# A gap of 448 bytes in front of the tiles that hold the lower weight parts of two transformer blocks

## The chip, the core and the metric

The kernel runs on one core of one Trainium2 chip. The metric is the device time of one execution in microseconds (us). Three runs of the kernel before took 2190.77, 2190.84 and 2191.94 us; their median is 2190.84 us. One further execution was profiled; it took 2190.65 us.

The engines are named as in the profile: PE is TensorE's matrix multiplication and PEld its loading of the stationary operand, DVE is VectorE, ACT is ScalarE, POOL is GpSimd, SP is SyncE, whose queue issues the loads from device memory.

## The reference, cut to what matters

Two transformer blocks over 256 positions of width 2048, in float32, one after the other. The first mixes a gated convolution, a pooling branch and a cross attention to 256 memory rows; the second has two kinds of attention. Both end in a gated feed-forward part of width 5632. Nearly all arithmetic is in products of the activations with weight matrices that are read once:

```python
h = rmsnorm(x, g_mix[l]);  z = h @ w_in[l]
...
x = x + mix @ w_out[l]
h = rmsnorm(x, g_ffn[l])
u = causal_dwconv(h @ w_up[l], ffn_conv_w[l]) + ffn_conv_b[l]
gate, val = jnp.split(u, 2, axis=-1)
x = x + (jax.nn.silu(gate) * val) @ w_down[l]
...
h = rmsnorm_2(x, norm_attn[l]);  proj = h @ w_in[l]
...
x = x + jnp.concatenate([ya, yb], axis=-1) @ w_out[l]
h = rmsnorm_2(x, norm_ffn[l])
x = x + (jax.nn.silu(h @ w_gate[l]) * (h @ w_up[l])) @ w_down[l]
return rmsnorm_2(x, norm_final)
```

## The kernel before, in words

**Number format.** A float32 weight `w` is split into an upper part `hi`, the value rounded to the format of TensorE's fast float32 mode (`float32r`), and a lower part `lo = w - hi`. Activations are split in the same way, and the two parts of an activation lie side by side: a row of tile `A` (and of `M`, `mix`, `hid`, `y`, which share one place) is 16 chunks of 512 columns, 256 of the upper part and 256 of the lower part. A product is then `hi` times both activation parts plus `lo` times the upper activation part.

**Units.** Weights come in units of 16 blocks of 128 x 128 (1 MB). SP's queue loads a unit into a tile `raw`, three units ahead. ScalarE copies half a unit (128 x 1024) into a tile `hi` (line 175); VectorE subtracts and writes the tile `lo` (line 187). There are three `raw` tiles and four each of `hi` and `lo`.

**The two kinds of matmul in most units** (function `products`, called by `ws_units`): weights are stationary, activations move. A *long* (line 208) loads a block of `hi` and moves the 512 columns of a chunk; a *short* (line 211) loads the block of `lo` and moves the first 256 columns of the same chunk:

```python
def long(acc, hi, lo, x, first, last):
    mm(acc, lhsT=hi, rhs=x, start=first, stop=last)

def short(acc, hi, lo, x, first, last):
    mm(acc[:, S:], lhsT=lo, rhs=x[:, :S], start=False, stop=False)
```

Blocks go four at a time, and `products` turns the order round from one four to the next, so that eight longs and eight shorts follow one another, except where a sum opens or closes.

**V units** (function `vs_unit`, lines 275 to 277): for the value projections the roles are exchanged. The activation slice is stationary and 512 columns of `hi` or `lo` move: line 275 loads the upper activation part and moves `hi`, 276 loads the same and moves `lo`, 277 loads the lower activation part and moves `hi`.

**Order.** Everything is written out by hand in `emit_all`: for each quarter of a unit the splits, the work that is due on the other engines (`post`), then the quarter's matmuls, then small products of the attention (`extra`). No scheduler moves anything.

**Places.** Tiles are allocated pool by pool, in the order in which the pools are made: `cst`, `wraw`, `whi`, `wlo`, `big`, then the small ones. The blocks of `hi` and `lo` are 512 bytes wide in a partition and the chunks of the activation tiles 2048 bytes, so all blocks of a kind, and all chunks, have the same place modulo 512 bytes. `big` begins with a tile of 64 bytes, `home`, that nothing uses. In the built program of the kernel before the places modulo 512 are: `raw`, `hi` and `lo` 32; `X`, `A` and the tile of `M`, `mix`, `hid` and `y` 96; the work tiles of the pools behind it (`z`, `c`, `qk` and others) 160; the table of constants `kc` 128.

Of the kernel before, what the change touches and what calls it, by code (L numbers as in the profile page):

```python
# [10 lines left out]
F32 = mybir.dt.float32  # L11
# [7 lines left out]
P = 128  # L19
# [80 lines left out]
def tile_two_blocks(ctx: ExitStack, tc: tile.TileContext, a: dict, out: bass.AP):  # L100
    nc = tc.nc
    pool = lambda name, bufs, **kw: ctx.enter_context(tc.tile_pool(name=name, bufs=bufs, **kw))
    cst = pool("cst", 1)
    wraw_p = pool("wraw", 3)
    whi_p = pool("whi", 4)
    wlo_p = pool("wlo", 4)
    big = pool("big", 1)
    t1 = pool("t1", 14)
# [10 lines left out]
    ones = cst.tile([P, P], F32, name="ones")  # L119
    ident = kc[:, K_IDENT:K_IDENT + P]  # L120

    big.tile([P, 16], F32, name="home")
    X = big.tile([P, KT, S], F32, name="X")
    A = big.tile([P, KT, 2 * S], F32R, name="A")
# [1006 lines left out]
```

## Time and profile before

| what | value |
|---|---|
| time, median of 3 runs | 2190.84 us |
| the profiled execution | 2190.65 us |
| its span, first to last instruction | 2188.8 us |
| PE busy | 2169.9 us, 99% |
| PEld busy | 1896.8 us, 87% |
| DVE busy | 1600.6 us, 73% |
| ACT busy | 1143.9 us, 52% |
| chain that ended last, on PE | 97% |

The profile lists, for each group of equal instructions, how many there are, the busy time that they cover together and the mean duration of one. Matmuls are pipelined, so the durations of neighbours overlap, and the sum of durations is more than the time. What a matmul costs in a row of them is seen in the chain that ended last: there each piece is given the time up to the start of the next one.

### The profile page before, as it was taken

What the parts mean: (1) busy time and instruction counts of PE and PEld (TensorE: products, weight loads), DVE (VectorE), ACT (ScalarE), POOL (GpSimd) and SP (SyncE); (2) the same over time, 40 slices, a digit from 0 to 9 for tenths busy, and PEclk for the clock granted to TensorE, in tenths of its full rate; (3) what the DMA queues carried; (4) which work ended last, traced back from release to release, by engine and by line L of the source; (5) the groups of instructions that cost most, each with busy time, mean ns of one, the idle gap of its engine ahead of it and who ended that gap; (6) DMA issues with size and microseconds to landing.
All of it is one profiled execution on the core that took longest, in us unless ns stands there. A gap on an engine that the chain in (4) does not pass through costs nothing.

```text
span 2188.8 us, 31334 instructions
## 1 busy us (share of the span) xinstructions
PE 2169.9 (99%) x12426; PEld 1896.8 (87%) x12426; DVE 1600.6 (73%) x2553; ACT 1143.9 (52%) x1738; POOL 108.2 (5%) x114
## 2 busy tenths in 40 slices
PE   8999999999999999999999999999999999999997
PEld 7888888888888888888888888888888888888886
DVE  8877778886588758888779677786665666666666
ACT  6555556664466535665456655455543445344442
POOL 4100010000000000003100000010000000000012
PEclk9999999999999999999999999999999999999998
DMA  7555555555555555555544444555555555555553
GB/s 284 201 171 180 191 188 196 191 192 191 193 192 192 193 184 193 190 185 192 193 167 160 156 172 154 175 199 189 191 190 193 193 192 193 192 192 189 189 184 113
DMA packets 60195, 408.99 MB, mean 187 GB/s; under 512 B 6672, under 2 KB 8592, under 8 KB 11792
## 3 DMA queue, kind: packets, MB, share of 16 engines
q1 hardware_dynamic: 60048, 406.99, 53.9%
q8 instruction: 97, 1.59, 0.3%
q14 instruction: 50, 0.41, 0.0%
HBM read 404.86 MB, written 2.10 MB: 186 GB/s over the span
## 4 chain that ended last, share of the span: by engine, by line
PE 97%; DVE 1%; DMA 1%; issue 0%; ACT 0%; DVEq 0%; SPq 0%; ACTq 0%
PE acc L208 60%; PE acc L211 30%; PE acc L275 1%; PE acc L276 1%; PE acc L277 1%; PE s_ps L432 1%; DMA raw<-in_w_k 1%; DVE lo L187 0%; PE pT_ps L468 0%; PE o_ps L922 0%; PE o_ps L880 0%; DVE M L545 0%; DVE end L1000 0%; DVE M L546 0%; PE nps L344 0%; DMA mem<-in_mem 0%
## 5 line engine op out<-in xcount | busy, mean ns | idle before, releaser
L175 ACT ACTIVATE hi<-raw 128x1024 fp32r<-128x1024 f32 x758 | 800.1, 1058 | 580.1 <-PE acc L208 405.5
L187 DVE TENSOR_TENSOR lo<-raw,hi 128x1024 fp32r<-128x1024 f32 x758 | 931.8, 1237 | 144.7 <-ACT hi L175 133.0
L208 PE MATMUL acc<-A,hi 128*128 128x512 f32 x3776 | 957.2, 393 | 0.0
L208 PEld LDWEIGHTS acc<-A,hi 128*128 128x128 f32 x3776 | 673.3, 188 | 115.5 <-issue 1.0
L211 PEld LDWEIGHTS acc<-A,lo 128*128 128x128 f32 x3776 | 509.3, 188 | 40.9 <-issue 0.7
L211 PE MATMUL acc<-A,lo 128*128 128x256 f32 x3776 | 523.4, 279 | 0.0
L208 PE MATMUL acc<-hid,hi 128*128 128x512 f32 x1408 | 360.1, 392 | 0.0
L208 PEld LDWEIGHTS acc<-hid,hi 128*128 128x128 f32 x1408 | 250.5, 188 | 41.4
L416 ACT ACTIVATE z<-acc 128x256 f32<-128x256 f32 x244 | 91.9, 382 | 262.4 <-PE acc L208 262.0
L211 PEld LDWEIGHTS acc<-hid,lo 128*128 128x128 f32 x1408 | 195.4, 188 | 17.3
L211 PE MATMUL acc<-hid,lo 128*128 128x256 f32 x1408 | 199.7, 279 | 0.0
L742 DVE TENSOR_TENSOR X<-acc,X 128x256 f32<-128x256 f32 x128 | 54.0, 422 | 177.4 <-PE acc L208 177.3
L418 DVE TENSOR_TENSOR z<-acc,z 128x256 f32<-128x256 f32 x244 | 103.1, 423 | 95.3 <-ACT z L416 89.6
L717 DVE SCALAR_TENSOR_TENSOR c<-z,vec,c 128x255 f32<-128x255 f32 (+1 forms) x188 | 90.0, 480 | 5.1 <-ACT c L712 1.1
L406 DVE TENSOR_TENSOR hid<-hid 128x256 fp32r<-128x256 f32 x88 | 37.4, 425 | 76.3 <-ACT hid L404 76.3
L424 DVE TENSOR_TENSOR z<-z,R_ffn 128x256 f32<-128x256 f32 x176 | 75.0, 426 | 6.0
L208 PE MATMUL acc<-y,hi 128*128 128x512 f32 x256 | 65.5, 394 | 0.0
L319 POOL TENSOR_TENSOR sq_attn<-sq_attn,sqt 128x256 f32<-128x256 f32 x30 | 29.5, 994 | 701.6 <-ACT sqt L317 701.5
L208 PE MATMUL acc<-mix,hi 128*128 128x512 f32 x256 | 64.2, 392 | 0.0
L394 ACT ACTIVATE A<-X,vec 128x256 fp32r<-128x256 f32 x64 | 32.5, 508 | 57.8 <-DVE X L743 57.3
L743 DVE TENSOR_TENSOR X<-acc,X 128x256 f32<-128x256 f32 x128 | 54.3, 425 | 4.4
L397 DVE SCALAR_TENSOR_TENSOR A<-X,vec,A 128x256 fp32r<-128x256 f32 x64 | 51.1, 810 | 8.3 <-ACT A L394 8.3
(174 smaller groups left out, 1352.6 us busy)
## 6 DMA issues: line engine op xcount, KB each, us to landing
raw<-in_w_up SPq DMA_DIRECT2D x88, 1024.0 KB, 4.8
raw<-in_w_down SPq DMA_DIRECT2D x88, 1024.0 KB, 4.9
raw<-in_w_gu SPq DMA_DIRECT2D x88, 1024.0 KB, 4.9
raw<-in_w_out SPq DMA_DIRECT2D x32, 1024.0 KB, 4.9
raw<-in_w_in SPq DMA_DIRECT2D x22, 1024.0 KB, 4.9
raw<-in_w_qkb SPq DMA_DIRECT2D x16, 1024.0 KB, 4.8
raw<-in_w_qka SPq DMA_DIRECT2D x16, 1024.0 KB, 4.9
raw<-in_w_vb SPq DMA_DIRECT2D x8, 1024.0 KB, 4.8
```

The source lines that it names most:

```text
L175: nc.scalar.activation(hi[:, :n], raws[i][:, c0:c0 + n], AF.Copy)
L187: nc.vector.tensor_tensor(out=lo[:, :n], in0=raws[i][:, c0:c0 + n], in1=hi[:, :n].bitcast(F32), op=ALU.subtract)
L208: mm(acc, lhsT=hi, rhs=x, start=first, stop=last)
L211: mm(acc[:, S:], lhsT=lo, rhs=x[:, :S], start=False, stop=False)
L397: nc.vector.scalar_tensor_tensor(out=a[:, kt, S:], in0=x, scalar=g, in1=hi.bitcast(F32), op0=ALU.mult, op1=ALU.subtract)
L406: nc.vector.tensor_tensor(out=hl[:, S:], in0=src, in1=h.bitcast(F32), op=ALU.subtract)
L416: nc.scalar.activation(z, acc[:, S:], AF.Copy)
L418: nc.vector.tensor_tensor(out=z, in0=acc[:, :S], in1=z, op=ALU.add)
L424: nc.vector.tensor_tensor(out=d, in0=z, in1=R, op=ALU.mult)
L717: nc.vector.scalar_tensor_tensor(out=c[:, s:], in0=z[:, :S - s], scalar=w[2 - s], in1=c[:, s:], op0=ALU.mult, op1=ALU.add)
L742: nc.vector.tensor_tensor(out=dst, in0=acc[:, :S], in1=X[:, m, :], op=ALU.add)
L743: nc.vector.tensor_tensor(out=dst, in0=acc[:, S:], in1=dst, op=ALU.add)
```

## The change

A pool `gap` with one tile of 112 float32 values (448 bytes in a partition) is made between `whi` and `wlo`. Nothing reads or writes it. All that lies behind it moves by 448 bytes, which is 64 less modulo 512. In the built program the places modulo 512 are then: `raw` and `hi` 32, as before; `lo` 480; `X`, `A` and the tile of `M`, `mix`, `hid` and `y` 32; the work tiles behind them 96; `kc` 128, as before. So the chunks of the activations lie like the blocks of `hi`, and both lie 64 bytes behind the blocks of `lo`. Before, the chunks lay 64 bytes behind the blocks of `hi` and of `lo`. The instructions, their order on every engine and their waits are the same.

```diff
@@ -103,6 +103,7 @@
     cst = pool("cst", 1)
     wraw_p = pool("wraw", 3)
     whi_p = pool("whi", 4)
+    gap = pool("gap", 1)
     wlo_p = pool("wlo", 4)
     big = pool("big", 1)
     t1 = pool("t1", 14)
@@ -119,6 +120,7 @@
     ones = cst.tile([P, P], F32, name="ones")
     ident = kc[:, K_IDENT:K_IDENT + P]
 
+    gap.tile([P, 112], F32, name="gap")
     big.tile([P, 16], F32, name="home")
     X = big.tile([P, KT, S], F32, name="X")
     A = big.tile([P, KT, 2 * S], F32R, name="A")
```

## Rows read from the trace of the kernel before

**Rows 1.** The page: busy time (share) xinstructions, granted clock by slice, chain's shares; clock.
```profile
PE 2169.9 (99%) x12426; PEld 1896.8 (87%) x12426; DVE 1600.6 (73%) x2553; ACT 1143.9 (52%) x1738; POOL 108.2 (5%) x114
...
PEclk9999999999999999999999999999999999999998
...
PE 97%; DVE 1%; DMA 1%; issue 0%; ACT 0%; DVEq 0%; SPq 0%; ACTq 0%
...
core 0: 2188.8 us, clock 0.997
```

**Rows 2.** Chain, 200 to 1000 us, by line; line 208's, then line 211's counts there.
```profile
by line: PE acc L208 66.3%; PE acc L211 33.6%; PE nps L344 0.1%; PE nps L326 0.0%
...
200.00:1000.00 800.00, 581.87 (x2317) 412.86 (x2316) 1.00 0.55 191
...
200.00:1000.00 800.00, 320.08 (x2318) 313.93 (x2318) 1.00 0.55 191
```

**Rows 3.** Lines 208 and 211, whole span: xcount, duration in ns min/median/max, first and last start.
```profile
L208 PE MATMUL acc<-A,hi x3776: 387/392/586, 58.9 to 2095.4; 128*128 128x512 f32 x199
...
L208 PE MATMUL acc<-hid,hi x1408: 387/392/397, 494.2 to 2172.9; 128*128 128x512 f32 x176
...
L208 PE MATMUL acc<-poolHL,hi x14: 387/392/396, 195.9 to 223.4; 128*128 128x512 f32 x14
...
L211 PE MATMUL acc<-A,lo x3776: 275/279/467, 59.8 to 2094.6; 128*128 128x256 f32 x199
```

**Rows 4.** Chain, 1597 to 1603 us: start us, us up to the next piece, what.
```profile
1597.11 0.91 PE acc L211 x8
1598.02 1.83 PE acc L208 x8
1599.84 0.94 PE acc L211 x8
```

**Rows 5.** Chain, 1066 to 1072 us, inside V units: by line, number of pieces, two of them.
```profile
by line: PE acc L276 35.0%; PE acc L277 35.0%; PE acc L275 34.9%
27 pieces in order of time: start us, us, what
...
1067.09 0.24 PE acc L277
1067.32 0.23 PE acc L275
```

**Rows 6.** Lines 275 to 277, as in rows 3, and what line 276's engine waited for.
```profile
L275 PE MATMUL acc<-hi,A x128: 393/398/497, 1046.5 to 1247.0; 128*128 128x512 f32 x128
...
L276 PE MATMUL acc<-lo,A x128: 388/396/399, 1046.7 to 1247.2; 128*128 128x512 f32 x128
...
  DVE lo L187: 5.0, 3
...
L277 PE MATMUL acc<-hi,A x128: 390/394/399, 1047.0 to 1247.5; 128*128 128x512 f32 x128
```

**Rows 7.** Timeline near 1015 us, matmuls, then loads: start us, us, engine, line, what, xcount.
```profile
1015.07 1.07 PE L208 MATMUL acc<-hid,hi 128*128 128x512 f32 x4
...
1014.96 0.76 PEld L208 LDWEIGHTS acc<-hid,hi 128*128 128x128 f32 x4
1015.76 0.19 PEld L211 LDWEIGHTS acc<-hid,lo 128*128 128x128 f32 x1
```

**Rows 8.** Chain at three places, as in rows 4.
```profile
1092.99 0.23 PE acc L277
...
1045.72 0.93 PE acc L208 x4
...
1281.10 0.91 PE acc L208 x4
1282.02 0.86 PE o_ps L880 x4
```

**Rows 9.** The lower parts' subtraction: group, xcount, busy us, mean ns, idle before.
```profile
L187 DVE TENSOR_TENSOR lo<-raw,hi 128x1024 fp32r<-128x1024 f32 x757 | 930.8, 1238 | 144.7 <-ACT hi L175 133.0
```

## The prediction

> **What bounds the kernel now.** I read the page first: TensorE is busy for 99% of the span, the chain that ended last lies on it for 97%, and its granted clock is full, 2.4 GHz, in all slices but the last (mean share 0.997) [rows 1]. VectorE has 27% of the span free and ScalarE 48%. So a nanosecond is worth something only where it is a nanosecond per matmul, and the next view is the chain inside a stretch, which gives the pitch of the matmuls: the time from the start of one to the start of the next. In the 800 us from 200 to 1000, line 208 (the long products, 512 moving columns) holds 66.3% of the chain in 2,317 instructions and line 211 (the short ones, 256 columns) 33.6% in 2,318 [rows 2]. That is 530.4 us / 2,317 = 228.9 ns for a long one and 268.8 us / 2,318 = 116.0 ns for a short one. The recorded durations, 392 and 279 ns in the median [rows 3], are longer by 163 ns since neighbours overlap; only differences of them count.
>
> The pitch is not one fixed number. A run of eight longs takes 1.83 us, 229 ns each, but a run of eight shorts takes 0.91 us (114 ns) in one place and 0.94 us (118 ns) in another, with the same tiles and shapes [rows 4]. Single long matmuls lie between 387 and 397 ns in duration [rows 3]. Nothing else waits there: something inside the matmul step, about 5 ns to either side, is open to change, and by 5,774 longs (seven groups by moving tile, of which the two largest and the last stand in [rows 3]) and as many shorts, 1 ns on every long is 5.8 us, 0.26% of the time.
>
> A third kind of step gives the comparison I rest on. In the V units (lines 275 to 277) the same 512-column matmul runs with the roles exchanged: the weight tile moves and the activation tile is loaded. There 27 steps fill 104.9% of 6 us [rows 5], so 233.1 ns, 4.2 ns more than in line 208; their medians of 398, 396 and 394 ns against 392 say the same [rows 3, 6]. What differs in addresses: in line 208 the moving tile lies 64 bytes behind the tile that is loaded beside it (places 96 and 32 modulo 512), in the V units 64 bytes ahead of it (32 and 96).
>
> **Rule against row.** By those rows the time of equal steps differs by 4.2 ns. The Trainium skill ("SBUF — State Buffer", Who interferes with whom, and "TensorE: Matmul & The Clock Gate", Step-by-step: what each phase is for) says that TensorE has two independent read ports, one for the moving operand and one for the weight load, and that a load takes nothing from the running matmul. By that rule placement is worth nothing and the sum would be zero; the trace does not bear it out fully, though it also exchanges the roles of the tiles.
>
> **The change part by part.** The instructions and their order on every engine are the same in both programs; only addresses move. Beside each matmul runs the load for the next one: a load that stands before four longs starts at 1014.96, 0.11 us ahead of the first of them (1015.07), and the load for the short behind them at 1015.76, when the fourth long starts (1015.07 + 3 x 0.229) [rows 7]. So what counts is the place of the running moving tile against the next stationary tile.
>
> *Longs beside a load of an upper part.* Most longs stand in runs of eight, some in runs of four [rows 4, 8], so about 7/8 of the 5,774 loads of upper parts run beside a long: 5,052 (an estimate). Here the distance goes from 64 bytes to 0. No run of the trace has 0; single steps have it. The last long before a V unit reads the activation tile while a slice of an activation tile is loaded: the four longs that end in it take 0.93 us at 1045.72, and again at another such place [rows 8], 232 ns each, one of them alike. The last V step before a long run reads the weight tile while a weight tile is loaded: 0.23 us, inside the V units' alternation of 0.23 and 0.24 [rows 5, 8]. Both are between the two levels and none shows a gain. I take the middle of the two levels, +2.1 ns: 5,052 x 2.1 = +10.6 us. The ends: the V level for all, +4.2 ns, +21.2 us; below, the fastest single step (387 against 392 ns, -5 ns), -25 us, which no run of eight comes near; a third of that, -8 us, is as far as I find likely.
>
> *Shorts beside a load of an upper part*, the other eighth, 722: distance 64 to 0. Their two levels are 114 and 118 around a mean of 116; I take 0, with ends of -2 x 722 = -1.4 and +2 x 722 = +1.4 us.
>
> *Everything beside a load of a lower part* (7/8 of the shorts, 1/8 of the longs): moving tile and lower tile both shift by -64 modulo 512 and keep their distance; 0. The one opening is the level that a run of shorts falls into, which is set at its start by something that the profile does not name. All at 114 would be 5,052 x -2 = -10 us, all at 118 +10 us.
>
> *V units.* Of three steps two (lines 275 and 277, upper part moving) come to distance 0, and line 276 keeps its own. 128 triples are bound by TensorE [rows 6], so 2 x 128 steps x -2.1 = -0.5 us; the 32 triples at the start wait for data, 0.
>
> *VectorE, ScalarE, DMA.* The subtraction that writes the lower part takes 1,238 ns, 757 times [rows 9]; its output moves against its inputs. I cost that at 0: line 276 waits for it three times, 5.0 us together [rows 6], and the chain from 200 to 1000 us has no wait for it. Were each 100 ns longer, VectorE would have 76 us more work and still over 500 us free. The scaling tables, which lie in front of the gap, move against the work tiles; that too is under VectorE's free time.
>
> **The sum** is made against the profiled execution, 2190.65 us, of which 2188.8 are the span: +10.6 - 0.5 = +10.1, 2200.8. The median of the three runs, 2190.84, is 0.2 above that execution: 2201 us.
>
> **Rivals.**
> 1. *Placement at this distance costs nothing.* For it: the single alike steps are within the spread of the others, and the V units' 4.2 ns may come from the exchanged roles rather than from the 64 bytes. Against it: those steps show no gain, and equal shapes do have two levels. Only the 0.5 us of the V units, or less, would be left: 2190 us. The rule of the two ports in the Trainium skill ("SBUF — State Buffer", Who interferes with whom) gives the same.
> 2. *Alike is better than 64 apart* (the other side). Mechanism: the load's reads and the moving reads, which start together, would then follow each other through the same places in step instead of meeting part way; the place is the 5,052 longs. For it: a long of 387 ns exists, so the step can be shorter by 5 ns; and the four longs at 1281.10, the last of which has a stationary tile alike beside it (the loaded values of line 880), take 0.91 us, 228 ns each [rows 8]. Against it: the fours before V units are at 0.93. At -2 ns on 5,052 longs the time is 2181 us. It decides from -0.9 ns per long, where 4.4 us are passed.
> 3. *The shorts change level.* The longs' new pitch shifts the moment at which a run of shorts begins, and more of them fall into the 114 ns level, or the 118 ns one: 2181 or 2201 us with the longs unchanged. For it: the same run shows both levels 3 us apart [rows 4]. Against it: the lower parts keep their distance.
> 4. *The change doesn't do what it says*: the built program has the places named, so this has no chance.
>
> **How the numbers follow.** A measurement of this kernel can tell about 0.2%, 4.4 us, from no change. The forecast, longs dearer by 1 ns up to the V level, has 0.48; rival 1 has 0.21; rival 2 has 0.20; rival 3 has 0.07 for the faster and 0.04 for the slower level. So slower 0.52, same 0.21, faster 0.27. The likeliest is 2201. Its own range is 2195 to 2213. The range for 8 in 10 takes in rival 1 and rivals 2 and 3 at the sizes given, 2180, and at the top the V level for the longs with small change elsewhere, 2213; beyond the ends I leave about 0.1 on each side.
>
> **What would show it.** In the changed kernel, the median duration of line 208's matmuls should go from 392 to about 394 ns, and a run of eight from 1.83 to about 1.85 us; line 211 should keep 279 ns in the median with runs of 0.91 and 0.94 us; lines 275 and 277 should fall from 398 and 394 by about 2 ns, and line 276 stay at 396. VectorE's and ScalarE's times should stay within a few ns. I am wrong in the main step if line 208 keeps 392 or falls, and wrong about the shorts if their share of the chain moves by more than 0.3% of the span.

## The result, and the profile after

| | median of the runs | runs | profiled execution | its span |
|---|---|---|---|---|
| before | 2191.03 us | 4 (2190.77 to 2191.94) | 2190.65 us | 2188.8 us |
| after | 2215.66 us | 4 (2215.28 to 2216.72) | 2215.45 us | 2213.6 us |

The changed kernel takes 1.0112 times as long, 95% interval 1.0095 to 1.013. The span grows by 24.8 us. The forecast was 2201 us and the top of its range 2213 us: the direction was right, the size was not.

The page of the changed kernel, its lines 210 and 213 being the longs and shorts (208 and 211 before), and line 189 the subtraction that writes the lower part:

```profile
PE 2194.1 (99%) x12426; PEld 1906.7 (86%) x12426; DVE 1603.3 (72%) x2553; ACT 1142.7 (52%) x1738; POOL 106.4 (5%) x114
...
PE 97%; DVE 1%; DMA 1%; SPq 0%; issue 0%; ACT 0%; DVEq 0%; ACTq 0%
...
L189 DVE TENSOR_TENSOR lo<-raw,hi 128x1024 fp32r<-128x1024 f32 x758 | 931.9, 1237 | 148.3 <-ACT hi L177 137.0
L210 PE MATMUL acc<-A,hi 128*128 128x512 f32 x3776 | 968.3, 396 | 0.0
...
L213 PE MATMUL acc<-A,lo 128*128 128x256 f32 x3776 | 531.1, 280 | 0.0
```

Against [rows 1, 9] only TensorE's rows have grown: the same 12,426 matmuls are busy for 24.2 us more (their loads, 188 ns each as before, cover 9.9 us more), the chain lies on PE for 97% as before, and the subtraction takes 1,237 ns, where it took 1,238. The mean granted clock is 0.997 in both. So the 24.8 us lie in the pitch of the matmuls. The chain from 200 to 1000 us by line, then the counts of line 210 and of line 213 there (us of the stretch, PE busy and count, PEld busy and count, clock, DMA share, GB/s):

```profile
by line: PE acc L210 66.3%; PE acc L213 33.6%; PE nps L346 0.1%; PE nps L328 0.0%
...
200.00:1000.00 800.00, 580.86 (x2285) 407.64 (x2285) 1.00 0.55 188
...
200.00:1000.00 800.00, 319.55 (x2283) 312.52 (x2282) 1.00 0.55 188
```

The shares are those of [rows 2]; the counts have fallen. A long takes 530.4 us / 2,285 = 232.1 ns, 3.2 more than before, and a short 268.8 us / 2,283 = 117.7 ns, 1.7 more. Over 5,774 of each that is +18.5 and +9.8 us. (Shares are printed to 0.1%, so each pitch is known to some 0.2 ns and each term to some 1 us.) The stretch gives the longs too much weight, however. Added up over the whole chain, the longs hold 1330.0 us, where they held 1315.6, the shorts 675.2 in place of 666.0, the V units' steps 94.5 in place of 96.2, and all the rest (small products and waits) 109.8 in place of 107.0. That is +14.4, +9.2, -1.7 and +2.8, together 24.7 of the 24.8 us.

In the chain near 1585 us (start, us up to the next piece, what) the two increases have a shape:

```profile
1585.53 1.86 PE acc L210 x8
1587.39 0.94 PE acc L213 x8
1588.33 1.82 PE acc L210 x8
```

Runs of eight longs, 1.83 us before [rows 4], take 1.86 and 1.82 us in turn in this stretch; runs of eight shorts, 0.94 and 0.91 us in turn before [rows 4], all take 0.94. In other long stretches the longs don't alternate:

```profile
701.91 1.87 PE acc L210 x8
703.78 0.94 PE acc L213 x8
704.73 1.87 PE acc L210 x8
```

Counted over the whole chain, 133 of 609 runs of eight longs take 1.82 to 1.84 us and 476 take 1.85 to 1.87, where all 609 took 1.83 or 1.84 before; of 624 runs of eight shorts 621 take 0.94 us, where 291 took 0.91 and 333 took 0.94. So one program, with one distance for all its longs, shows several levels.

The V units went the other way. The chain from 1080 to 1086 us, and lines 277 to 279 (min/median/max duration in ns), which were 275 to 277:

```profile
by line: PE acc L278 34.7%; PE acc L277 34.4%; PE acc L279 33.9%
27 pieces in order of time: start us, us, what
...
L277 PE MATMUL acc<-hi,A x128: 387/390/500, 1059.1 to 1258.7; 128*128 128x512 f32 x128
...
L278 PE MATMUL acc<-lo,A x128: 392/392/400, 1059.3 to 1258.9; 128*128 128x512 f32 x128
...
L279 PE MATMUL acc<-hi,A x128: 388/389/400, 1059.5 to 1259.2; 128*128 128x512 f32 x128
```

27 steps fill 103.0% of 6 us, 228.9 ns each, where they took 233.1 [rows 5]; the medians fell from 398, 396 and 394 ns [rows 6] to 390, 392 and 389. That is 384 x -4.2 = -1.6 us. With the terms of the one stretch the sum would be 18.5 + 9.8 - 1.6 = 26.7 us, above the 24.8 measured; the sums over the whole chain, above, are the better account.

### The profile page after: what moved, and what is told of

It is laid out like the page before. It is cut to its first block, busy times and chain, and to the rows that moved or that the text cites. A ratio compares the mean times of both kernels' runs of the same rounds, so it can differ in the third digit from the quotient of the medians.

```text
span 2213.6 us, 31334 instructions
## 1 busy us (share of the span) xinstructions
PE 2194.1 (99%) x12426; PEld 1906.7 (86%) x12426; DVE 1603.3 (72%) x2553; ACT 1142.7 (52%) x1738; POOL 106.4 (5%) x114
## 4 chain that ended last, share of the span: by engine, by line
PE 97%; DVE 1%; DMA 1%; SPq 0%; issue 0%; ACT 0%; DVEq 0%; ACTq 0%
PE acc L210 60%; PE acc L213 30%; PE acc L277 1%; PE acc L278 1%; PE acc L279 1%; PE s_ps L434 1%; DMA raw<-in_w_k 1%; DVE lo L189 0%; PE pT_ps L470 0%; PE o_ps L924 0%; PE o_ps L882 0%; DVE M L547 0%; DVE end L1002 0%; DVE M L548 0%; PE nps L346 0%
## 5 line engine op out<-in xcount | busy, mean ns | idle before, releaser
L189 DVE TENSOR_TENSOR lo<-raw,hi 128x1024 fp32r<-128x1024 f32 x758 | 931.9, 1237 | 148.3 <-ACT hi L177 137.0
L210 PE MATMUL acc<-A,hi 128*128 128x512 f32 x3776 | 968.3, 396 | 0.0
L213 PEld LDWEIGHTS acc<-A,lo 128*128 128x128 f32 x3776 | 515.4, 188 | 42.9 <-issue 0.7
L213 PE MATMUL acc<-A,lo 128*128 128x256 f32 x3776 | 531.1, 280 | 0.0
L420 DVE TENSOR_TENSOR z<-acc,z 128x256 f32<-128x256 f32 x244 | 103.0, 422 | 104.8 <-ACT z L418 103.6
```

Source lines behind the costliest of these rows:

```text
L189: nc.vector.tensor_tensor(out=lo[:, :n], in0=raws[i][:, c0:c0 + n], in1=hi[:, :n].bitcast(F32), op=ALU.subtract)
L420: nc.vector.tensor_tensor(out=z, in0=acc[:, :S], in1=z, op=ALU.add)
```

## The experiments: is it the distance, the place, or the roles?

*Distance* is, as in the prediction, the moving tile's place less that of the stationary tile that is loaded beside it, modulo 512 bytes. My theory at this point: the distance sets the pitch. Rivals: the absolute places do; or the longs became dear because of what else moved. All four kernels leave the instructions and their order alone. On the chip of these four the kernel before took 2189.82 us. All times of experiments from here on are of one execution each unless the count is given; those of the kernel before lie between 2189.8 and 2191.9 us.

**All tiles moved, distances as before.** The gap of 448 bytes goes in front of `hi`, so that `hi` and `lo` lie at 480 and the activations at 32:

```diff
+    front = pool("front", 1)
     whi_p = pool("whi", 4)
...
+    front.tile([P, 112], F32, name="front")
     big.tile([P, 16], F32, name="home")
```

> All distances as in the kernel before, all places shifted by -64 modulo 512 (upper and lower parts at 480, moving tiles at 32 as in the changed kernel). Theory A (the distance between the moving tile and the tile loaded beside it decides): 2191 us, line of the long products at 392 ns median, runs of shorts at 0.91 and 0.94 us. Theory B (the place of the moving tiles themselves decides, 96 good and 32 bad): 2215 us, medians 396 and 280 as in the changed kernel.

It took 2192.6 us. Its page rows (lines 210 and 213 are the longs and shorts) and its chain:

```profile
L210 PE MATMUL acc<-A,hi 128*128 128x512 f32 x3776 | 957.3, 393 | 0.0
L213 PE MATMUL acc<-A,lo 128*128 128x256 f32 x3776 | 523.4, 279 | 0.0
...
1585.28 0.94 PE acc L213 x8
1586.22 1.83 PE acc L210 x8
1588.05 0.91 PE acc L213 x8
```

These are the runs of [rows 4], with the activations at 32 as in the changed kernel; over the whole chain 294 runs of shorts take 0.91 us and 330 take 0.94, against 291 and 333 in the kernel before. The absolute places are not the cause; what is left of the addresses is the distances.

**All three alike** (distance 0 to the upper and the lower parts; `home` left out of the kernel before, longs and shorts on lines 207 and 210):

```diff
-    big.tile([P, 16], F32, name="home")
```

> The tile of 64 bytes in front of the moving tiles is left out: upper parts, lower parts and moving tiles all at 32, so both distances are 0. Theory A: longs cost at least what they cost in the changed kernel (396 ns median) and shorts are alike too, so 2215 us or more, up to 2225. Theory C (only the upper parts' distance matters, the shorts follow from the moment at which the longs let them start): 2215 us, as the changed kernel. If the lower parts' 64 bytes were what hurt in the changed kernel: below 2205 us.

**Only the lower parts alike** (upper distance 64 as before, lower 0; lines 209 and 212):

```diff
+    gap = pool("gap", 1)
     wlo_p = pool("wlo", 4)
...
-    big.tile([P, 16], F32, name="home")
+    gap.tile([P, 16], F32, name="gap")
```

> Upper parts 64 bytes from the moving tiles as in the kernel before (32 and 96), lower parts alike with the moving tiles (96). Theory A: longs stay at 392 ns median, the shorts lose their lower level and take 118 ns each, +10 us: 2201 us. Theory C: longs and shorts as before, 2191 us. If alike is what costs for shorts as much as for longs (3 ns on each): 2207 us.

**The longs at the V units' distance** (upper distance -64, lower 64 as before; `hi` 160, `lo` 32, activations 96; lines 212 and 215):

```diff
+    front = pool("front", 1)
     whi_p = pool("whi", 4)
+    gap = pool("gap", 1)
...
+    front.tile([P, 32], F32, name="front")
+    gap.tile([P, 96], F32, name="gap")
```

> Upper parts 64 bytes on the other side of the moving tiles (160 and 96), lower parts as before (32 and 96). This gives the longs the distance that the V steps have in the kernel before, and the V steps with an upper part moving the distance that the longs have there. Theory A: longs at the V level, 233 ns (median 396 ns), V steps at 229 ns: 2191 + 5,774 x 4.2 ns = 2215 us. If the V level comes from the exchanged roles: longs stay at 229 ns, 2191 us.

All three lost: 2211.34, 2208.92 and 2218.44 us. The first is below the 2215 us that two theories named, the second above theory A's 2201 and near the last case's 2207, the third 3 us above theory A's 2215. The chain of the first:

```profile
1583.17 0.95 PE acc L210 x8
1584.12 1.84 PE acc L207 x8
```

of the second:

```profile
1585.19 0.96 PE acc L212 x8
1586.15 1.83 PE acc L209 x8
```

and of the third:

```profile
1583.59 1.86 PE acc L212 x8
1585.45 0.94 PE acc L215 x8
```

Three things follow. With the distance of the V units the longs take their time, 1.86 / 8 = 232.5 ns against 233.1 [rows 5]: so the 4.2 ns that the prediction rested on need no exchanged roles; the distance is enough. At distance 0 in both kinds a run of longs takes 1.84 us (568 of 609 runs): "alike" is not in itself worth the changed kernel's 1.86 and 1.87. And in the third kernel the shorts, whose distance is that of the kernel before, take 0.94 or 0.95 us, and in the second the longs, whose distance is kept, take 1.85 us in 358 of 609 runs: a step whose own distance is kept loses when its neighbours change. That last point says that a step's own distance is not all. (In the second and third kernel, as in the changed one, the distance between the upper and the lower parts changed as well; no run here separates that.)

## The experiments: is it the moment at which a run starts?

Theory now: a distance offers more than one pitch, and the moment at which a run starts, which the run before it sets, picks one. Rival: the pitch is a mean that belongs to the pair of distances, and a shifted start changes nothing but the work left out. To move the start alone, the last long ahead of a run of shorts is cut by 8 of its 512 columns (688 times), once in the kernel before and once in the changed one. The products of these 8 columns are left out. At (229 - 116) / 256 = 0.44 ns a column, that is 688 x 3.5 ns = 2.4 us less work in either. The same edit in both:

```diff
+        def cut(acc, hi, lo, x, first, last):
+            mm(acc[:, :504], lhsT=hi, rhs=x[:, :504], start=False, stop=False)
+
...
-            for b in opening + between:
+            for b in opening + between[:-1]:
                 long(*b)
+            for b in between[-1:]:
+                cut(*b)
             for b in blocks:
```

In the kernel before:

> The kernel before, with the long matmul that stands just ahead of a run of shorts moving 504 columns instead of 512 (the last 8 columns of that product are left out, some 700 times), so that each run of shorts starts about 3 ns earlier against the rest; all distances as before. By itself that is 700 x 3.3 ns = -2.3 us. Theory D (the distance sets which pitches are possible, the moment at which a run starts picks one of them): the shares of runs of eight shorts at 0.91 and at 0.94 us, about half and half before, change clearly, towards all of one kind: 2181 or 2199 us. If the start has no say: shares as before, 2188 us.

In the changed kernel:

> The same cut of 8 columns in the changed kernel, where all runs of shorts are at 0.94 us or a little over. Theory D: a share of the runs of shorts comes back to 0.91 us, or the longs' runs (1.82 to 1.87 us) change their shares; the time moves by 5 to 15 us from 2215, to either side. If the start has no say: 2213 us with unchanged runs.

With 2190.90 us for the kernel before on this chip, the two took 2200.87 and 2193.74 us. The chain of the first (line 211 is the cut long, 214 the shorts):

```profile
1583.01 1.60 PE acc L208 x7
1584.61 0.23 PE acc L211
1584.84 0.94 PE acc L214 x8
```

and of the second (line 213 is the cut long, 216 the shorts):

```profile
1583.81 1.60 PE acc L210 x7
1585.41 0.22 PE acc L213
1585.63 0.94 PE acc L216 x8
```

In the kernel before, less work costs 10 us. Of 624 runs of shorts 614 now take 0.94 us, where 333 did. Over the whole chain the shorts hold 10.5 us more than before, and the longs with the cut ones 0.1 us less: a run with a cut takes 1.60 + 0.23 = 1.83 us, as it did without, so the 8 columns left out gave nothing back. All distances are those of the kernel before, so a shifted start can by itself bring the shorts to 0.94 us. In the changed kernel the same cut gives back 22 us of the 24.8, of which 2.4 are the work left out, and more than the 5 to 15 us that I expected. There it is the longs that change: 469 of 609 runs now take 1.60 + 0.22 = 1.82 us, where 129 did, and over the whole chain the longs with the cut ones hold 18.2 us less, the shorts 1.1 us less. The distance of the changed kernel is the same in both, and with the same cut in both kernels the changed one is the faster by 7 us. So the loss of the changed kernel is not a fixed price of its distance: it depends on the moments at which its runs happen to start. This is shown for the longs; the shorts of the changed kernel stay at 0.94 us in 568 of 624 runs.

**Twice the cut, 16 columns,** in the changed kernel, which tells an effect that grows with the cut from one that returns (the edit with 496 for 504; those 16 columns are left out):

> The changed kernel with the long ahead of a run of shorts moving 496 columns instead of 512 (16 columns of that product left out, 688 times; 4.6 us less work). Theory D with a period of 16 columns (6.67 ns, 64 bytes of a row): a cut of 16 puts the start of the shorts back to the same moment as no cut, so runs of longs and shorts keep the shares of the changed kernel and only the work goes: 2211 us. If an earlier start helps by itself, as the cut of 8 (2194 us) could also be read: 2190 us or less.

2216.39 us, the changed kernel's own time again, although about 4.8 us of work are gone:

```profile
1584.27 1.64 PE acc L210 x7
1585.90 0.23 PE acc L213
```

Longs at 234 ns again (1.64 / 7), in 563 of 609 runs. So 8 columns help and 16 do not: the effect of the cut does not grow with it, the loss returns. A period of 16 columns is the simplest reading, but the shares are not those of the changed kernel (46 runs at 1.60 to 1.62 us, where 133 of its runs were fast) and the time is 5 us above what I expected, so the return is shown and the period is only suggested.

## The experiments: which distances are good?

If distance decides what levels there are, a map of it should have structure: does it repeat, and is 64 special? In the kernel before, only the size of `home` is changed, so that both distances, upper and lower, move together (32 shown; 8, 24, 56 and 64 values give distances of 32, 96, 224 and 256 bytes):

```diff
-    big.tile([P, 16], F32, name="home")
+    big.tile([P, 32], F32, name="home")
```

> Both distances 128 bytes instead of 64 (upper and lower parts at 32, moving tiles at 160). Theory A (only the distance counts, and it counts modulo more than 64): pitches that are neither those of 64 nor those of 0; the nearest rows, the few steps on the pooled tiles with this distance (median 392 ns, 280 ns), say 2191 to 2200 us. If only 64 against 0 or the other side matters: 2191 us.

> Both distances 256 bytes, half of a weight block, as far from alike as can be. Theory A with reads that meet when they lie close: no meeting at the start, meeting half way; 2185 to 2200 us. If distances repeat with a short period of 128 or 256 bytes it equals the all-alike kernel, 2211 us.

> Both distances 32 bytes (upper and lower parts at 32, moving tiles at 64). The distance sets the possible pitches, so a set of its own is to be expected; between alike (2211 us) and 64 (2191 us) by distance: 2200 us. If distances matter in steps of 64 bytes alone: like one of its neighbours, 2191 or 2211 us.

> Both distances 96 bytes (moving tiles at 128), between 64 (2191 us) and 128 (2223 us): 2207 us by distance; if 64-byte steps alone matter, 2191 or 2223 us.

> Both distances 224 bytes (moving tiles at 256), which is 32 on the other side if distances repeat every 256 bytes, as the equal times of 0 and 256 say. Between alike (2211 us) and the other side's 64 (longs at 233 ns): 2205 to 2220 us.

| both distances, bytes | time, us | before on that chip | run of 8 longs, us | run of 8 shorts, us |
|---|---|---|---|---|
| 0 (above) | 2211.34 | 2189.82 | 1.84 | 0.95 |
| 32 | 2217.55 | 2191.61 | 1.87 | 0.93 |
| 64 (kernel before) | 2191.03 | | 1.83 | 0.94 and 0.91 |
| 96 | 2236.91 | 2191.61 | 1.87 | 0.96 |
| 128 | 2223.54 | 2190.90 | 1.86 and 1.87 | 0.94 and 0.95 |
| 224 | 2226.74 | 2191.61 | 1.86 | 0.95 |
| 256 | 2212.85 | 2190.90 | 1.84 | 0.95 |

The last two columns are of the stretch near 1585 us alone. The page of distance 256 and that of distance 0 have the same rows for the longs and shorts, to the last digit (the kernel of 256 first; the other lies two or one lines earlier in its file, lines 207 and 210):

```profile
L208 PE MATMUL acc<-A,hi 128*128 128x512 f32 x3776 | 961.4, 394 | 0.0
L211 PE MATMUL acc<-A,lo 128*128 128x256 f32 x3776 | 535.0, 283 | 0.0
```

```profile
L207 PE MATMUL acc<-A,hi 128*128 128x512 f32 x3776 | 961.4, 394 | 0.0
L210 PE MATMUL acc<-A,lo 128*128 128x256 f32 x3776 | 535.0, 283 | 0.0
```

So the distances 0 and 256 act as one distance; that others repeat after 256 bytes too was not tried. The four distances between them that were new came out slower than any time I had named for them (2200 us for 128, 2211 for 32, 2223 for 96, 2220 for 224). There is no simple slope: 96, which lies between 64 and 128, is the worst of all, 45 us above the kernel before, and 32 has the slowest longs with nearly the fastest shorts. The chain of 96 and of 32:

```profile
1584.50 0.96 PE acc L211 x8
1585.46 1.87 PE acc L208 x8
```

```profile
1583.29 1.87 PE acc L208 x8
1585.16 0.93 PE acc L211 x8
```

Of the six different distances tried, 64 is the best by 20 us and more, in the order of instructions that this kernel has. Whether it is better by itself or by luck of the moments, this table can't tell, since each entry has moments of its own.

## The experiments: moving the moment with all work kept

The last test keeps every product. The last short ahead of a run of longs (699 of them) is written to the first half of the accumulator, which is added to the second in the end anyway, and moves a few columns more than 256, the first columns of the lower activation part. That adds some of the product of the two lower parts, which the kernel otherwise leaves out, and delays the next run of longs by a little. With 8 columns:

```diff
+        def more(acc, hi, lo, x, first, last):
+            mm(acc[:, :S + 8], lhsT=lo, rhs=x[:, :S + 8], start=False, stop=False)
+
...
-            for b in blocks:
+            for b in blocks[:-1]:
                 short(*b)
+            (more if between and not opening else short)(*blocks[-1])
```

4, 8 and 12 columns in the kernel before, and 8 in the changed one (2190.78 us for the kernel before on this chip):

> The kernel before with nothing left out: the last short ahead of a run of longs moves 260 columns instead of 256 (it also multiplies the lower weight part with 4 columns of the lower activation part, a term that belongs to the exact product), 699 times, +1.2 us of work. Distances as before. Theory D: the longs start at another moment, end at another, and the runs of shorts change their shares of 0.91 and 0.94 us: between 2181 (all at 0.91) and 2201 us (all at 0.94). If starts have a say only through shorter work: 2192 us with half and half.

> As the last one with 8 columns more (264), +2.3 us of work, half of the 16-column period. Theory D: shares of the runs of shorts change again, and not as with 4: between 2182 and 2202 us. Without a say of the start: 2193 us.

> As the last two with 12 columns more (268), +3.5 us of work. Theory D: between 2183 and 2203 us, with another share. Without a say of the start: 2194 us.

> The changed kernel with nothing left out and the last short ahead of a run of longs moving 264 columns, +2.3 us of work. Theory D: the alike distance is not dear by itself, its longs can run at 227.5 ns when they start at a good moment, as they did behind the cut of 8; this puts the longs' start half a period later: most runs of longs at 1.82 us, 2198 us. If the alike distance itself costs: 2218 us.

They took 2200.77, 2212.38, 2185.61 and 2204.68 us. The chain with 8 columns more and with 12 more, both in the kernel before (line 211 is the widened short, 214 the others):

```profile
1585.13 1.85 PE acc L208 x8
1586.98 0.82 PE acc L214 x7
```

```profile
1583.56 0.79 PE acc L214 x7
1584.36 0.12 PE acc L211
1584.48 1.83 PE acc L208 x8
```

With 4 columns more, and with 8 more in the changed kernel (line 210 the longs there):

```profile
1584.88 0.82 PE acc L214 x7
```

```profile
1585.57 1.84 PE acc L210 x8
```

The added work is 1.2, 2.5 and 3.7 us (699 x 0.44 ns x columns, an estimate). What is measured is +10, +21.6 and -5.2 us; +21.6 is 10 us above the range named for 8 columns, which had left the longs as they were. The three differ in nothing but the number of columns, so the other half of the accumulator, which all three write, is not what separates them; what that half does by itself was not measured. With 4 columns most shorts (592 of 624 runs) are at 0.82 / 7 = 117 ns; with 8 the longs, too, rise from 1.83 to 1.85 us (544 of 609 runs); with 12 the shorts fall to 0.79 / 7 = 113 ns in 568 of 624 runs. In the changed kernel, where the cut helped, 8 columns more help as well, by 11 us: 573 of 609 runs of longs take 1.84 us, not the 1.82 hoped for. Its shorts stay at 117 ns (0.82 / 7).

**The version that is faster than both.** 12 columns more in the kernel before, timed over nine executions, and the same in the changed kernel:

> The kernel before with the last short ahead of a run of longs moving 268 columns, all work done, timed in five rounds against the kernel before. One look said 2185.6 against 2190.8 us: a ratio of 0.9976, if it holds.

> The changed kernel with the last short ahead of a run of longs moving 268 columns, +3.5 us of work. Theory D: other shares than with 8 columns more (2204.7 us). If shorts reach 0.91 us per run and longs stay near 1.84: 2186 us; if the shorts stay at 0.94: 2200 to 2220 us.

In the kernel before it takes 2185.53 us (9 runs, 2183.97 to 2187.87) against 2190.85 (13 runs): 0.9974 times, 95% interval 0.9964 to 0.9984. Its chain from 200 to 1000 us, and the counts of lines 208, 214 and 211 there:

```profile
by line: PE acc L208 66.6%; PE acc L214 29.1%; PE acc L211 4.2%; PE nps L348 0.1%; PE nps L330 0.0%
...
200.00:1000.00 800.00, 584.22 (x2323) 414.94 (x2322) 1.00 0.56 191
...
200.00:1000.00 800.00, 284.54 (x2046) 279.58 (x2046) 1.00 0.56 191
...
200.00:1000.00 800.00, 79.04 (x280) 52.57 (x280) 1.00 0.56 191
```

In this stretch longs take 532.8 / 2,323 = 229.4 ns, 0.5 more than in [rows 2]. The shorts take 232.8 / 2,046 = 113.8, the widened ones 33.6 / 280 = 120.0, together 114.5 in place of 116.0. Over 5,774 of each that is +2.9 - 8.7 = -5.8 us, beside -5.3 measured in the median. (The profiled execution was the slowest of the nine, 2187.87 us. Over its whole chain the longs hold 1.2 us more than in the kernel before and the shorts 6.7 less, the rest 2.8 more.) It is a version to know of rather than a design: the gain hangs on the moments of this one order of instructions. In the changed kernel the same edit gives 2212.34 us, 3 us below the changed kernel and far from the kernel before.

Side by side (one execution each, except 2185.53 and the first row), the starts alone decide whether the gap of 448 bytes costs or gains:

| the starts | before, us | changed, us | the gap's price, us |
|---|---|---|---|
| as they are | 2191.03 | 2215.66 | +24.6 |
| 8 columns cut | 2200.87 | 2193.74 | -7.1 |
| 8 columns more | 2212.38 | 2204.68 | -7.7 |
| 12 columns more | 2185.53 | 2212.34 | +26.8 |

## Why the prediction was right or wrong, point by point

*What bounds the kernel* was right: the longs and shorts, whose pitch alone has changed, hold 23.6 of the 24.8 us more, and the rows of VectorE, ScalarE and the DMA queue show no part in it. The costs of nothing put on them held (the subtraction takes 1,237 ns). Term by term over the whole chain, the forecast of +10.1 us became 24.7: longs +14.4 in place of +10.6, shorts +9.2 in place of 0, V units -1.7 in place of -0.5, the rest +2.8 in place of 0. (In the kernel with all tiles shifted, whose distances are those of before, the rest holds 104.5 us, 2.5 less than before; so its +2.8 is of the size by which it varies anyway.)

*Everything beside the load of a lower part*: this is the step that failed most, 0 where +9.2 us were measured. The opening named in the prediction, rival 3 on its slower side, is what happened: all but 3 of 624 runs of shorts are at 0.94 us, though their distance was kept. The prediction gave it 0.04, and priced it rightly, at +10 us. The argument against it ("the lower parts keep their distance") was the error. With every distance kept, a cut of 8 columns in the kernel before brings the shorts to 0.94 us, so a step that is untouched can still lose its better level when the step before it changes. That this is how it came about in the changed kernel is likely but not shown: with four other starts there its shorts stay near 0.94 us, so something else that the gap changed, such as the distance between upper and lower parts, may hold them there.

*Longs beside the load of an upper part*: that the pitch depends on the distance was right, and so was the side. The size failed: +10.6 us, the middle of two levels, for +14.4. The step that failed is the taking of a middle from single steps. Fours of longs that end in an alike step were read as a price of distance 0, but one such four, at 1281.10, takes 0.91 us [rows 8], and in the kernel before fours without such a step take the same 0.93 us:

```profile
818.78 0.93 PE acc L208 x4
819.70 0.94 PE acc L211 x8
```

And in the changed program runs of eight at distance 0 take from 1.82 to 1.87 us, while with an 8-column cut most take 1.82. There is no one price; the sign depends on where the run starts. So the right side was partly luck: with 8 columns more in both kernels the changed one is the faster. Rival 2's fast runs (228 ns) exist, as 129 of 609 runs here; its 0.20 was for a case that a cut comes near and the change alone does not.

*V units*: the sign was right, the size was not: -4.2 ns on three steps, -1.6 us, in place of -2.1 on two. Line 276 (now 278), whose distance was kept, fell with the others: again an untouched step put at nothing.

*Rival 1, placement costs nothing*, is out. The Trainium skill's two independent read ports ("SBUF — State Buffer", Who interferes with whom) would have made the kernel before and the four of the first series equal; they differ by up to 29 us on one chip. On what a load itself takes the rule isn't touched by that: the runs here speak of the pitch of the matmuls alone, which changes by up to 5 ns with the tiles' places.

*What would show it*: the median of line 210 went from 392 to 396 ns and runs to 1.82, 1.86 and 1.87 us, where 394 and 1.85 were named. The test for the shorts, by their share of the chain, was a bad one: the share stayed at 33.6%, as both kinds grew, and only the counts showed the rise.

**Left open.** Why the start of a run picks a level isn't shown by any row; the runs show that shifting it changes the levels. What of the changed kernel's shorts belongs to their start, and what to other distances that moved, is open. Whether the tile that matters is the one being loaded or the one loaded before can't be told here, as all blocks of a kind have the same place modulo 512. Distances of 160 and 192 bytes, and other pairs of upper and lower distances than those above, were not tried.

## What to carry to other kernels

Where a kernel is bound by back-to-back matmuls, the pitch from the chain and its counts, by kind of step, is the quantity to read, and addresses alone can move it, here by up to 2% of the time: treat the distance between moving and stationary tiles as a parameter to be swept (here 0 and 256 bytes were alike), and don't infer its price from single steps, nor the levels of a whole kernel from one stretch. When such a pitch has two levels in one trace, an edit to one kind of step can tip the others, as the start did here, so a cost of nothing for an untouched step needs a reason beyond "it is untouched". Experiments that shift a start by a few columns, in both versions, tell a fixed price from a price of the moment.

## What was unexpected

- Places alone, with the same instructions in the same order, make times from 2190 to 2237 us, 2.1%.
- 0 and 256 bytes give the same rows to the last digit (961.4 us, 394 ns; 535.0 us, 283 ns).
- Less work was slower (8 columns less, 688 times: +10 us) and more work faster (12 columns more, 699 times: -5.3 us), while 8 columns more cost 21.6 us.
- The same gap costs 25 to 27 us with two starts and gains 7 to 8 us with two others.
